# RMSNorm with Silu on one core: program order pinned on every engine, square-sums three tiles ahead, every fourth square-sum on VectorE

## The chip, the core and the metric

The kernel runs on one core of one Trainium2 chip. The metric is the device time of one execution in microseconds (us); the median of three runs is given. The core's engines used here are ScalarE (ACT in the profile), VectorE (DVE), GpSimd (POOL) and SyncE (SP), whose queue issues all transfers between device memory (HBM) and the on-chip memory (SBUF). TensorE does nothing in this kernel.

## The reference

```python
# x: (8, 1024, 2048) float32, gamma: (2048,) float32, eps: float32(1e-5)
rms = np.sqrt(np.mean(x ** 2, axis=-1, keepdims=True) + eps)
out = gamma * x / rms
return (out * (1 / (1 + np.exp(-out)))).astype(np.float32)
```

Each row of 2048 numbers is divided by its root mean square, multiplied by gamma and passed through Silu. Input and output are 67 MB each.

## The kernel before

The 8192 rows are cut into 64 tiles of 128 rows by 2048 columns, float32, 1 MB each. A tile lives in one buffer of a pool `xt` of 23 buffers from its load to its store: it is scaled and passed through Silu in place.

For a tile i there are four steps.

- `load(i)` (line 41) issues a DMA from x to a buffer on SP's queue.
- `stats(i)`: line 59 is a Square on ScalarE, which writes the squares to a scratch tile `sq` that nobody reads and accumulates the row sums into `ss` (on the chip this is the activation and a small accumulator read behind it). Lines 61 and 64 on GpSimd turn the row sum into `var` = mean + eps and `rstd` = var to the power of -0.5; both work on a single column of 128 numbers.
- `scale(i)` (line 68) is one VectorE instruction over the whole tile: x times `rstd` times `g`, in place. `g` is gamma copied to all 128 partitions by GpSimd at the start (line 47).
- `finish(i)`: line 73 is the Silu on ScalarE, in place; line 74 issues the store of the tile on SP's queue; then `load(i+16)` is issued on the same queue.

Sixteen loads are issued at first (`LEAD` = 16). The main loop's turn i calls `stats(i)`, `scale(i-1)` and `finish(i-2)`. The order in which each engine receives its instructions is not this order as written: a scheduler in the framework places them, with the program's dependences as its limits, and each engine then works through its own list in order. The engines wait for one another by semaphores.

Of the kernel before, what the change touches and what calls it, by code (L numbers as in the profile page):

```python
# [1 line left out]

# [4 lines left out]

ACT = mybir.ActivationFunctionType
ALU = mybir.AluOpType


@with_exitstack
def kernel(
    ctx: ExitStack,
    tc: tile.TileContext,
    x: bass.AP,
    gamma: bass.AP,
    eps: bass.AP,
    out: bass.AP,
):  # L20


    nc = tc.nc
    P = nc.NUM_PARTITIONS
    bf16 = mybir.dt.bfloat16
    f32 = mybir.dt.float32
    x2 = x.flatten_outer_dims()
    o2 = out.flatten_outer_dims()
    n, d = x2.shape
    ntiles = n // P  # L30
    BUFS, LEAD = 23, 16

    singles = ctx.enter_context(tc.tile_pool(name="singles", bufs=1))
    pool = ctx.enter_context(tc.tile_pool(name="pool", bufs=BUFS))
    small = ctx.enter_context(tc.tile_pool(name="small", bufs=8))

    xts = {}

    def load(i):
        xt = pool.tile([P, d], f32, name="xt")  # L40
        nc.sync.dma_start(out=xt, in_=x2[i * P:(i + 1) * P])
        xts[i] = xt

    grow = singles.tile([1, d], f32)
    nc.sync.dma_start(out=grow, in_=bass.AP(tensor=gamma.tensor, offset=gamma.offset, ap=[[d, 1], gamma.ap[0]]))
    g = singles.tile([P, d], f32)
    nc.gpsimd.partition_broadcast(g, grow)  # L47
    half = singles.tile([P, 1], f32)
    nc.gpsimd.memset(half, -0.5)  # L49
    sq = singles.tile([P, d], bf16)  # L50

    for i in range(LEAD):
        load(i)

    rstds = {}

    def stats(i):
        ss = small.tile([P, 1], f32, name="ss")
        nc.scalar.activation(out=sq, in_=xts[i], func=ACT.Square, accum_out=ss)  # L59
        var = small.tile([P, 1], f32, name="var")  # L60
        nc.gpsimd.tensor_scalar(out=var, in0=ss, scalar1=1.0 / d, scalar2=float(eps),  # L61
                                op0=ALU.mult, op1=ALU.add)
        rstd = small.tile([P, 1], f32, name="rstd")
        nc.gpsimd.tensor_tensor(out=rstd, in0=var, in1=half, op=ALU.pow)  # L64
        rstds[i] = rstd

    def scale(i):
        nc.vector.scalar_tensor_tensor(out=xts[i], in0=xts[i], scalar=rstds.pop(i), in1=g,  # L68
                                       op0=ALU.mult, op1=ALU.mult)

    def finish(i):
        xt = xts.pop(i)
        nc.scalar.activation(out=xt, in_=xt, func=ACT.Silu)  # L73
        nc.sync.dma_start(out=o2[i * P:(i + 1) * P], in_=xt)
        if i + LEAD < ntiles:
            load(i + LEAD)

    for i in range(ntiles + 2):
        if i < ntiles:
            stats(i)  # L80
        if 0 <= i - 1 < ntiles:
            scale(i - 1)
        if i >= 2:
            finish(i - 2)


# [1 line left out]
_INS = ['x', 'gamma', 'eps']  # L88
_OUTS = [((8, 1024, 2048), 'float32')]

_NUMBERS = {'eps': 9.999999747378752e-06}


# [26 lines left out]
```

## Time and profile before

| | |
|---|---|
| median of 3 runs | 413.59 us (413.02 to 413.94) |
| the profiled execution | 412.76 us; its span from first to last instruction 410.8 us |
| ScalarE busy | 244.6 us, 60% of the span |
| VectorE busy | 150.4 us, 37% |
| GpSimd busy | 60.1 us, 15% |
| moved by DMA | 134.28 MB, mean 327 GB/s over the span |

The profile describes one execution. Its page cuts the span in 40 equal slices of 10.27 us; a digit is the busy share of an engine in that slice in tenths, and the row GB/s tells what the 16 DMA engines moved. A list of waits names who waited for whom, in total and at the longest; the timeline lists instructions by start, duration, engine, line and operation, with the idle time ahead of one in brackets, and what ended it. Times inside the profile count from the start of the span; an execution takes 1.96 us more than its span here (412.76 less 410.8).

### The profile page before, as it was taken

What the parts mean: (1) busy time and instruction counts of PE and PEld (TensorE: products, weight loads), DVE (VectorE), ACT (ScalarE), POOL (GpSimd) and SP (SyncE); (2) the same over time, 40 slices, a digit from 0 to 9 for tenths busy, and PEclk for the clock granted to TensorE, in tenths of its full rate; (3) what the DMA queues carried; (4) which work ended last, traced back from release to release, by engine and by line L of the source; (5) the groups of instructions that cost most, each with busy time, mean ns of one, the idle gap of its engine ahead of it and who ended that gap; (6) DMA issues with size and microseconds to landing.
All of it is one profiled execution on the core that took longest, in us unless ns stands there. A gap on an engine that the chain in (4) does not pass through costs nothing.

```text
span 410.8 us, 895 instructions
## 1 busy us (share of the span) xinstructions
DVE 150.4 (37%) x64; ACT 244.6 (60%) x194; POOL 60.1 (15%) x134
## 2 busy tenths in 40 slices
DVE  0067666634242323324424233232424233242422
ACT  4549999984636465554763645556463645546462
POOL 1176212210010101010201010101001010101100
DMA  7999999999999999999999987887844242424334
GB/s 308 419 424 422 416 426 427 425 428 426 427 428 427 428 426 428 427 428 428 428 427 428 365 303 298 300 312 281 295 179 165 112 194 102 204 102 166 140 136 171
DMA packets 18440, 134.28 MB, mean 327 GB/s; under 512 B 2049, under 2 KB 2049, under 8 KB 2049
## 3 DMA queue, kind: packets, MB, share of 16 engines
q1 hardware_dynamic: 18434, 134.23, 80.0%
q14 instruction: 6, 0.05, 0.0%
HBM read 67.12 MB, written 67.11 MB: 327 GB/s over the span
## 4 chain that ended last, share of the span: by engine, by line
issue 76%; POOL 10%; DVE 1%; ACT 0%; POOLq 0%
POOL rstd L64 7%; POOL var L61 3%; DVE xt L68 1%; ACT xt L73 0%; POOLq L64 0%; POOLq L115 0%; ACT sq L59 0%
## 5 line engine op out<-in xcount | busy, mean ns | idle before, releaser
L68 DVE SCALAR_TENSOR_TENSOR xt<-xt,rstd,g 128x2048 f32<-128x2048 f32 x64 | 150.4, 2352 | 253.7 <-POOL rstd L64 252.9
L73 ACT ACTIVATE xt<-xt 128x2048 f32<-128x2048 f32 x64 | 121.7, 1905 | 155.1 <-DVE xt L68 154.0
L59 ACT ACTIVATE sq<-xt 128x2048 bf16<-128x2048 f32 x64 | 121.2, 1894 | 5.7 <-DMA xt<-in_x_dram 5.6
L61 POOL TENSOR_SCALAR var<-ss 128x1 f32<-128x1 f32 x64 | 20.4, 319 | 327.6 <-ACT sq L59 316.1
L64 POOL TENSOR_TENSOR rstd<-var,half 128x1 f32<-128x1 f32 x64 | 37.0, 579 | 5.4 <-POOL var L61 0.2
L59 ACT ACTIVATION_READ_ACCUMULATOR sq<-xt 128x1 f32 x64 | 11.9, 186 | 0.0
L47 POOL PARTITION_BROADCAST g<-grow x1 | 2.3, 2302 | 8.2 <-issue 8.2
L59 ACT ACT_TABLE_LOAD x1 | 1.3, 1283 | 0.7 <-PEq L101 0.7
L73 ACT ACT_TABLE_LOAD x1 | 1.3, 1283 | 0.0
L49 POOL MEMSET half<- 128x1 f32 x1 | 0.1, 99 | 0.3 <-POOLq L101 0.3
L101 POOL MEMSET const-float32-0.0<- 128x1 f32 x1 | 0.1, 98 | 0.2 <-issue 0.2
L101 POOL MEMSET const-bfloat16-1.0<- 128x1 bf16 x1 | 0.1, 101 | 0.0
L101 POOL MEMSET const-uint8-127<- 128x1 uint8 x1 | 0.1, 101 | 0.0
L101 POOL MEMSET const-float32-1.0<- 128x1 f32 x1 | 0.1, 99 | 0.0
## 6 DMA issues: line engine op xcount, KB each, us to landing
xt<-in_x_dram SPq DMA_DIRECT2D x64, 1024.0 KB, 19.6
out_dram<-xt SPq DMA_DIRECT2D x64, 1024.0 KB, 18.2
grow<-in_gamma_dram SPq DMA_DIRECT2D x1, 8.0 KB
```

The costliest lines, as they stand in the source:

```text
L47: nc.gpsimd.partition_broadcast(g, grow)
L49: nc.gpsimd.memset(half, -0.5)
L59: nc.scalar.activation(out=sq, in_=xts[i], func=ACT.Square, accum_out=ss)
L61: nc.gpsimd.tensor_scalar(out=var, in0=ss, scalar1=1.0 / d, scalar2=float(eps), op0=ALU.mult, op1=ALU.add)
L64: nc.gpsimd.tensor_tensor(out=rstd, in0=var, in1=half, op=ALU.pow)
L68: nc.vector.scalar_tensor_tensor(out=xts[i], in0=xts[i], scalar=rstds.pop(i), in1=g, op0=ALU.mult, op1=ALU.mult)
L73: nc.scalar.activation(out=xt, in_=xt, func=ACT.Silu)
L101: nc = _bacc.Bacc("TRN2", target_bir_lowering=False, num_devices=1)
```

## The change

Everything from the load of gamma to the last store stands inside `tc.manual_schedule()`: each engine gets its instructions in the order of the program's text. The loop is rewritten: `stats` of tiles 0, 1, 2 come first, and turn i then calls `stats(i+3)`, `scale(i)`, `finish(i-1)`. In `stats`, tiles with i % 4 == 3 take their square-sum by one VectorE instruction, whose elementwise result goes to a scratch tile `junk` in PSUM; the others stay on ScalarE, with two scratch tiles `sq` in turn. For the second `sq` the pool `xt` has 22 buffers and `LEAD` is 15.

```diff
-    BUFS, LEAD = 23, 16
+    BUFS, LEAD = 22, 15
...
+    psum = ctx.enter_context(tc.tile_pool(name="psum", bufs=1, space=bass.MemoryType.PSUM))
...
+    with tc.manual_schedule():
...
-    sq = singles.tile([P, d], bf16)
+        sq = [singles.tile([P, d], bf16, name=f"sq{k}") for k in range(2)]
+        junk = psum.tile([P, d], f32)
...
         def stats(i):
             ss = small.tile([P, 1], f32, name="ss")
-        nc.scalar.activation(out=sq, in_=xts[i], func=ACT.Square, accum_out=ss)
+            if i % 4 == 3:
+                nc.vector.tensor_tensor_reduce(out=junk, in0=xts[i], in1=xts[i], scale=1.0, scalar=0.0,
+                                               op0=ALU.mult, op1=ALU.add, accum_out=ss)
+            else:
+                nc.scalar.activation(out=sq[i % 2], in_=xts[i], func=ACT.Square, accum_out=ss)
...
-    for i in range(ntiles + 2):
-        if i < ntiles:
+        for i in range(3):
             stats(i)
-        if 0 <= i - 1 < ntiles:
-            scale(i - 1)
-        if i >= 2:
-            finish(i - 2)
+        for i in range(ntiles):
+            if i + 3 < ntiles:
+                stats(i + 3)
+            scale(i)
+            if i >= 1:
+                finish(i - 1)
+        finish(ntiles - 1)
```

The code of `var`, `rstd`, `scale` and `finish` is the same, further to the right. On GpSimd's queue the text puts the broadcast of gamma ahead of the memset of `half`.

More of the change, by code (lines that the diff above doesn't have):

```diff
@@ L42, in load @@
         xts[i] = xt
[L44 to L49, printed above, removed]
-    sq = singles.tile([P, d], bf16)
[L52 to L76, printed above, removed]
-    for i in range(ntiles + 2):
-        if i < ntiles:
-            stats(i)
-        if 0 <= i - 1 < ntiles:
-            scale(i - 1)
-        if i >= 2:
-            finish(i - 2)
+    with tc.manual_schedule():
+        grow = singles.tile([1, d], f32)
+        nc.sync.dma_start(out=grow, in_=bass.AP(tensor=gamma.tensor, offset=gamma.offset, ap=[[d, 1], gamma.ap[0]]))
+        g = singles.tile([P, d], f32)
+        nc.gpsimd.partition_broadcast(g, grow)
+        half = singles.tile([P, 1], f32)
+        nc.gpsimd.memset(half, -0.5)
+        sq = [singles.tile([P, d], bf16, name=f"sq{k}") for k in range(2)]
+        junk = psum.tile([P, d], f32)
+        for i in range(LEAD):
+            load(i)
+        rstds = {}
+        def stats(i):
+            ss = small.tile([P, 1], f32, name="ss")
+            if i % 4 == 3:
[3 more added lines that the diff above has]
+                nc.scalar.activation(out=sq[i % 2], in_=xts[i], func=ACT.Square, accum_out=ss)
+            var = small.tile([P, 1], f32, name="var")
+            nc.gpsimd.tensor_scalar(out=var, in0=ss, scalar1=1.0 / d, scalar2=float(eps),
+                                    op0=ALU.mult, op1=ALU.add)
+            rstd = small.tile([P, 1], f32, name="rstd")
+            nc.gpsimd.tensor_tensor(out=rstd, in0=var, in1=half, op=ALU.pow)
+            rstds[i] = rstd
+        def scale(i):
+            nc.vector.scalar_tensor_tensor(out=xts[i], in0=xts[i], scalar=rstds.pop(i), in1=g,
+                                           op0=ALU.mult, op1=ALU.mult)
+        def finish(i):
+            xt = xts.pop(i)
+            nc.scalar.activation(out=xt, in_=xt, func=ACT.Silu)
+            nc.sync.dma_start(out=o2[i * P:(i + 1) * P], in_=xt)
+            if i + LEAD < ntiles:
+                load(i + LEAD)
+        for i in range(3):
+            stats(i)
+        for i in range(ntiles):
[5 more added lines that the diff above has]
+        finish(ntiles - 1)
```

## The prediction

> **What bounds the kernel now.** I read the page's slices first, then a table by stretches of time, then the waits and the timeline of one stretch, then the SP queue.
>
> ```profile
> span 410.8 us, 895 instructions
> GB/s 308 419 424 422 416 426 427 425 428 426 427 428 427 428 426 428 427 428 428 428 427 428 365 303 298 300 312 281 295 179 165 112 194 102 204 102 166 140 136 171
> DMA packets 18440, 134.28 MB, mean 327 GB/s; under 512 B 2049, under 2 KB 2049, under 8 KB 2049
> ...
> 0.00:10.27 10.27, 0.00 (x0) 4.92 (x4) 1.56 (x6) 1.00 0.78 308
> 10.27:84.00 73.73, 42.23 (x18) 63.23 (x54) 23.70 (x38) 1.00 1.01 423
> 84.00:226.00 142.00, 49.39 (x21) 79.49 (x63) 16.40 (x42) 1.00 1.01 427
> 226.00:300.00 74.00, 23.52 (x10) 40.72 (x32) 7.37 (x20) 1.00 0.84 304
> 300.00:411.00 111.00, 35.28 (x15) 56.19 (x45) 11.06 (x30) 1.00 0.37 151
> ```
>
> The rows of stretches give length, busy time of VectorE, ScalarE and GpSimd, clock, DMA share and GB/s. Up to 226 us the 16 DMA engines are full at 423 to 428 GB/s. After that they are not: 304, then 151. So the first 226 us are bound by transfers and the last 185 us by something else; ScalarE, busy 40.72 of 74 us and 56.19 of 111, isn't it.
>
> ```profile
> 277.69 1.89 ACT L59 ACTIVATE sq<-xt 128x2048 bf16<-128x2048 f32 x1
> 279.49 0.19 ACT L59 ACTIVATION_READ_ACCUMULATOR sq<-xt 128x1 f32 x1
> 279.77 0.19 POOL L61 TENSOR_SCALAR var<-ss 128x1 f32<-128x1 f32 x1 [6.31 <-ACT sq L59]
> 280.04 0.55 POOL L64 TENSOR_TENSOR rstd<-var,half 128x1 f32<-128x1 f32 x1
> 280.62 2.35 DVE L68 SCALAR_TENSOR_TENSOR xt<-xt,rstd,g 128x2048 f32<-128x2048 f32 x1 [4.78 <-POOL rstd L64]
> 283.01 1.91 ACT L73 ACTIVATE xt<-xt 128x2048 f32<-128x2048 f32 x1 [3.33 <-DVE xt L68]
> 284.82 1.89 ACT L59 ACTIVATE sq<-xt 128x2048 bf16<-128x2048 f32 x1
> ```
>
> This is a ring: Square, var, rstd, scale, Silu, and only behind that Silu the next tile's Square. It turns in 284.82 - 277.69 = 7.13 us, each engine waiting for the one before it. The scheduler's order does it: the Silu of a tile stands on ScalarE directly behind that tile's own Square. The waits from 84 us on, a query over that stretch, agree:
>
> ```profile
> DVE xt L68 <- POOL rstd L64: 212.5, 46, 4.9
> ACT xt L73 <- DVE xt L68: 144.5, 44, 3.5
> ```
>
> The ring sets the pace from 84 us on, but until 226 us transfers queued ahead hide it. Before 84 us another order held, in which ScalarE never waited and a tile took 3.7 us (rows below).
>
> **The change, part by part.**
>
> *The new order.* ScalarE gets Square(i+3), then Silu(i-1). Silu(i-1) depends on a Square issued four turns earlier, so the ring is open and each engine can run at its own rate. That rate, from these rows:
>
> ```profile
> 32.04 1.89 ACT L73 ACTIVATE xt<-xt 128x2048 f32<-128x2048 f32 x1
> 33.84 1.89 ACT L59 ACTIVATE sq<-xt 128x2048 bf16<-128x2048 f32 x1
> 35.74 1.89 ACT L73 ACTIVATE xt<-xt 128x2048 f32<-128x2048 f32 x1
> ...
> L68 DVE SCALAR_TENSOR_TENSOR xt<-xt,rstd,g 128x2048 f32<-128x2048 f32 x64 | 150.4, 2352 | 253.7 <-POOL rstd L64 252.9
> ```
>
> From start to start a Silu takes 33.84 - 32.04 = 1.80 us and a Square 35.74 - 33.84 = 1.90. Per four tiles ScalarE then has 4 x 1.80 + 3 x 1.90 = 12.9 us, 3.23 a tile (3.70 with all Squares).
>
> *The square-sum on VectorE.* No row shows this operation, nor VectorE writing PSUM. Bounds: 1.90 us (the same work on ScalarE) and 4.70 (two passes as long as a scale). I take 2.35, the scale, which also reads two full float32 operands on the same engine. VectorE then has 4 x 2.35 + 2.35 = 11.8 us per four tiles, 2.94 a tile; with the upper bound 3.53.
>
> *GpSimd beside VectorE.* These two block each other:
>
> ```profile
> 28.74 2.35 DVE L68 SCALAR_TENSOR_TENSOR xt<-xt,rstd,g 128x2048 f32<-128x2048 f32 x1 [0.44 <-POOL rstd L64]
> 28.79 2.35 POOL L61 TENSOR_SCALAR var<-ss 128x1 f32<-128x1 f32 x1
> 31.23 0.55 POOL L64 TENSOR_TENSOR rstd<-var,half 128x1 f32<-128x1 f32 x1
> ```
>
> A `var` of 0.19 us took 2.35 beside a scale. At worst the two engines work strictly in turn: 2.94 + 0.19 + 0.55 = 3.68 us a tile (4.27 with the upper bound). Scale(i) needs an rstd whose square-sum is three turns old, so a `var` that waits out one VectorE instruction delays nothing.
>
> *Transfers.* A tile is two transfers of 1.049 MB; at 427 GB/s 2 x 2.456 = 4.91 us. That is above 3.23, 2.94, 3.68 and 4.27: the transfers become the bound all the way, if SP always has the next one to issue. Its queue:
>
> ```profile
> 1.12 23.27 SPq L41 DMA_DIRECT2D xt<-in_x_dram  x16
> 13.61 1.91 ACT L59 ACTIVATE sq<-xt 128x2048 bf16<-128x2048 f32 x1 [0.47 <-DMA xt<-in_x_dram]
> 22.52 0.45 POOL L61 TENSOR_SCALAR var<-ss 128x1 f32<-128x1 f32 x2 [11.22 <-issue]
> 23.69 4.61 DVE L68 SCALAR_TENSOR_TENSOR xt<-xt,rstd,g 128x2048 f32<-128x2048 f32 x2 [23.69 <-POOL rstd L64]
> 26.07 1.91 ACT L73 ACTIVATE xt<-xt 128x2048 f32<-128x2048 f32 x1 [9.16 <-DVE xt L68]
> 28.01 0.34 SPq L74 DMA_DIRECT2D out_dram<-xt  x1
> ...
> SPq L74 <- ACT xt L73: 203.4, 34, 6.7
> SPq L41 <- DMA xt<-in_x_dram: 80.0, 40, 2.7
> ...
> xt<-in_x_dram SPq DMA_DIRECT2D x64, 1024.0 KB, 19.6
> ```
>
> A load lands 19.6 us after its issue, 8 x 2.456: eight transfers are under way at a time, and SP waits for the oldest. Now the places where it could run dry.
>
> At the start the path to the first store is unchanged: it hangs on GpSimd's first `var` at 22.52, before which nothing that the profile shows holds it back, and I keep that start. Scale(0) follows at 23.7, Silu(0) at 26.07, store(0) at 28.01. The new VectorE square-sum of tile 3, ahead of scale(0), starts when its load lands near 13.6 and is done by 16 (18.3 by the upper bound). Square(4), ahead of Silu(0), is done near 18. Moving the memset of `half` behind the broadcast costs 0.1 us under that same gap: nothing. One load fewer: load 14 lands at 13.6 + 11 x 2.456 = 40.6, so the DMA engines have work until then and the first store comes 12.6 us sooner. From there a pair of store and load is offered each 3.7 us and eaten each 4.91: the queue is back at eight within some 25 us.
>
> In the steady state load(i+15), issued behind store(i), lands eight transfers later, about when store(i+4) is issued. Silu(j) follows Square(j+4) on ScalarE, so it runs when load(j+4) is there; load(j+4) went out behind store(j-11) and lands about at store(j-7). Store(j) is thus ready some six pairs, 29 us, before its turn. The store's wait, behind which the next load is queued on SP, costs nothing; if that cover went, it would be the 203.4 us row again. A load reuses the buffer of tile i-7, whose store was issued 15 transfers earlier and landed with eight under way. So 22 buffers cost nothing, nor does the second `sq`: Squares follow in order on one engine anyway.
>
> At the end load(63) lands with 15 stores to go, 36.8 us of transfers. VectorE then does its square-sum and four scales, 11.8 us, then Silu(63), 1.9: some 14 us after the landing, with up to 3 for GpSimd 17. Store(63) may be issued at 7 x 2.456 = 17.2. Covered, and eight under way give another 19.6.
>
> *The sum.* From the stretches: 308 x 10.27 + 423 x 73.73 + 427 x 142 = 95.0 MB by 226 us, at the full rate already. The remaining 39.3 MB at 427 GB/s take 92.0 us: 318.0. The last store of before shows what follows the last byte:
>
> ```profile
> 409.00:409.50 0.50, 0.00 (x0) 0.00 (x0) 0.00 (x0) 1.00 0.67 279
> 409.50:410.00 0.50, 0.00 (x0) 0.00 (x0) 0.00 (x0) 1.00 0.01 0
> DMA to landing us min/median/max: 3.9/3.9/4.0
> ```
>
> Bytes stop near 409.5, the span ends at 410.8: 1.3 us. So the span is 319.3 and the execution 1.96 more, 321.3. The profiled execution, 412.76, lies 0.83 under the median: 322. With 423 GB/s after 84 us instead of 427, 99.9 MB take 2.2 us more; with 430, 1.6 less.
>
> The DMA row against a rule: 428 GB/s stood for slice after slice. The Trainium skill, DMA: Bandwidth & Descriptors, section Where 436 GB/s comes from, says that for transfers between HBM and SBUF the HBM side binds, at about 358 GB/s for a core. By that the whole would take an estimated 375 us of transfer, some 381 in all; the trace, at 427 with loads and stores mixed, disagrees.
>
> **Rivals.**
>
> *A. Stores alone are slower.* The last 15 stores run without loads. A lone store lands 3.9 us after issue (row above); 15 of those instead of 2.456 add 21.7 us: 344. This would show as slices near 270 GB/s at the end. Against it: between its first and last byte it moved at full rate, and the initial loads, alone, ran at 419 to 424. 4%.
>
> *B. The rate isn't held when all engines work.* The lowest row with a nearly full queue is 365 GB/s, in the slice where it ran dry. The remaining 39.3 MB at that rate take 107.7 us: 338; all at 365: about 375. Against it: 10.27 to 84 us, with ScalarE 86% busy, still gave 423. 3%. The skill's rule just named would end here, at about 381.
>
> *C. VectorE becomes the bound.* In strict turns with GpSimd, a tile passes 4.91 us once the square-sum exceeds 4 x 4.91 - 4 x (2.35 + 0.74) = 7.3 us. Each us above costs 16 us; at 10 us the time is 322 + 43 = 365. For it: no row times this operation. 3%.
>
> *D. Slower: SP's queue goes one at a time.* With the order pinned, a load stands behind a store that waits for a Silu. Were each transfer to wait for the one before to land, a pair would take at least 2 x 3.9 = 7.8 us: 64 x 7.8 = 499. It decides from 6.3 us a pair, 64 x 6.3 = 403. Against it: SP's waits for loads are 2.0 us each (80.0 in 40), less than one transfer. 2%.
>
> *E. The ring stays.* If ScalarE still got a tile's Silu right behind its Square, the pace of 7.13 us and 413 us would stay. Against it is only that the text's order is what each engine gets. 1%.
>
> **How the numbers follow.** The forecast has 87%, A to E 4, 3, 3, 2 and 1. The forecast's own span is 319 to 326: transfer rate 430 to 423, start and end a few us worse. 318 to 330 leaves out the rivals and little else. A measurement can tell about 0.2% (0.8 us; the runs of before spread by that much). Faster 97%, within 0.2% 1%, slower 2%.
>
> **What would show it.** GB/s near 425 in every slice from the second to the last but one; ScalarE about 69% busy (48 Squares, 64 Silus), waiting mostly for loads; VectorE 64 scales and 16 square-sums near 2.35 us, 188 us or near 59%; SP waiting for DMAs in nearly every wait and hardly for Silu; the ring's two waits of 6.31 and 4.78 us gone. The prediction is wrong if GB/s sags late (A, B), if the square-sum takes over 7 us (C), or if SP waits for Silu (D, E).

## The result, and the profile after

The changed kernel takes 323.58 us (median of four runs, 323.25 to 323.70) against 413.30 for the kernel before beside it (412.90 to 413.94): a ratio of 0.783, 95% interval 0.781 to 0.784. The forecast was 322, range 318 to 330. The profiled execution has a span of 321.8 us, 2.5 more than the 319.3 of the sum.

From the page of the changed kernel: span, busy rows, slices, queue.

```profile
span 321.8 us, 812 instructions
DVE 183.8 (57%) x96; ACT 213.2 (66%) x162; POOL 185.5 (58%) x134
...
GB/s 273 428 415 424 399 426 428 428 423 428 426 432 424 425 427 432 424 426 427 433 426 426 427 430 428 425 428 429 428 425 428 428 431 424 428 426 432 424 428 233
...
q1 hardware_dynamic: 18434, 134.23, 99.2%
```

All slices but the first and the last stand between 399 and 433 GB/s, and all but two of these at 423 or more; the 18 low slices at the end of the kernel before are gone. The queue's packets fill 99.2% of the 16 DMA engines' span (80.0% before). The kernel is bound by transfers over nearly the whole span; how it ends is taken up below.

The waits of the engines, and below them those of SP's queue (total us, times, longest):

```profile
DVE junk L64 <- DMA xt<-in_x_dram: 88.7, 11, 13.6
ACT sq L67 <- DMA xt<-in_x_dram: 61.6, 30, 4.2
...
DVE xt L76 <- POOL rstd L72: 22.5, 25, 7.3
ACT xt L81 <- DVE xt L76: 17.1, 10, 6.2
...
SPq L82 <- DMA out_dram<-xt: 118.5, 56, 2.9
SPq L43 <- DMA xt<-in_x_dram: 110.5, 54, 2.7
...
SPq L82 <- ACT xt L81: 7.5, 6, 3.6
```

The ring's waits have shrunk from 252.9 to 22.5 us (scale for rstd) and from 154.0 to 17.1 (Silu for scale). VectorE and ScalarE now wait mostly for loads. SP waited 203.4 us for Silus before and waits 7.5 now; otherwise it waits some 2 us each time for the oldest of the transfers under way.

The groups by line:

```profile
L76 DVE SCALAR_TENSOR_TENSOR xt<-xt,rstd,g 128x2048 f32<-128x2048 f32 x64 | 147.9, 2349 | 22.5 <-POOL rstd L72 22.5
L69 POOL TENSOR_SCALAR var<-ss 128x1 f32<-128x1 f32 x64 | 100.4, 1569 | 91.5 <-DVE ss L64 39.3
L64 DVE CUSTOM_DVE_ANT_0 junk<-xt 128x2048 f32<-128x2048 f32 x16 | 36.8, 2298 | 88.7 <-DMA xt<-in_x_dram 88.7
L64 DVE DVE_READ_ACCUMULATOR2_ANT ss<- 128x1 f32 x16 | 2.3, 142 | 0.0
```

The square-sum on VectorE takes 2.30 us and 0.14 for reading the accumulator. A `var` on GpSimd, 0.32 us on average before, takes 1.57 now, since most of them run beside an instruction of VectorE. VectorE's whole wait for `rstd` is 22.5 us, and the transfers, not VectorE, set the pace, so that costs next to nothing here.

### The profile page after: what moved, and what is told of

Read it like the earlier page. It is cut to its first block, busy times and chain, and to the rows that moved or that the text cites. A ratio compares the mean times of both kernels' runs of the same rounds, so it can differ in the third digit from the quotient of the medians.

```text
span 321.8 us, 812 instructions
## 1 busy us (share of the span) xinstructions
DVE 183.8 (57%) x96; ACT 213.2 (66%) x162; POOL 185.5 (58%) x134
## 3 DMA queue, kind: packets, MB, share of 16 engines
q1 hardware_dynamic: 18434, 134.23, 99.2%
## 5 line engine op out<-in xcount | busy, mean ns | idle before, releaser
L76 DVE SCALAR_TENSOR_TENSOR xt<-xt,rstd,g 128x2048 f32<-128x2048 f32 x64 | 147.9, 2349 | 22.5 <-POOL rstd L72 22.5
L69 POOL TENSOR_SCALAR var<-ss 128x1 f32<-128x1 f32 x64 | 100.4, 1569 | 91.5 <-DVE ss L64 39.3
L67 ACT ACTIVATE sq<-xt 128x2048 bf16<-128x2048 f32 x48 | 91.4, 1904 | 65.9 <-DMA xt<-in_x_dram 61.6
L81 ACT ACTIVATE xt<-xt 128x2048 f32<-128x2048 f32 x64 | 120.0, 1897 | 17.1 <-DVE xt L76 17.1
L64 DVE CUSTOM_DVE_ANT_0 junk<-xt 128x2048 f32<-128x2048 f32 x16 | 36.8, 2298 | 88.7 <-DMA xt<-in_x_dram 88.7
L72 POOL TENSOR_TENSOR rstd<-var,half 128x1 f32<-128x1 f32 x64 | 82.5, 1290 | 5.3
L67 ACT ACTIVATION_READ_ACCUMULATOR sq<-xt 128x1 f32 x48 | 8.9, 186 | 0.0
L64 DVE DVE_READ_ACCUMULATOR2_ANT ss<- 128x1 f32 x16 | 2.3, 142 | 0.0
```

The source lines that it names most:

```text
L64: nc.vector.tensor_tensor_reduce(out=junk, in0=xts[i], in1=xts[i], scale=1.0, scalar=0.0, op0=ALU.mult, op1=ALU.add, accum_out=ss)
L67: nc.scalar.activation(out=sq[i % 2], in_=xts[i], func=ACT.Square, accum_out=ss)
```

## The experiments

**How much of the gain is the order, and how much the square-sums taken off ScalarE?** The order alone:

```diff
-            if i % 4 == 3:
+            if False:
```

> All 64 square-sums stay on ScalarE; the order and everything else is the changed kernel's. Theory 'order': ScalarE at 1.80 + 1.90 = 3.70 us a tile is still faster than the two transfers of a tile at 4.91 us, so the time is that of the changed kernel, 323 to 325 us. Rival 'relief': if a part of the gain came from the 16 square-sums taken off ScalarE, the time goes up by up to 16 x 1.9 = 30 us, to 330 to 354 us.

Measured: 323.05 us (322.81 to 323.19), ratio 0.782 (0.780 to 0.783) to the kernel before. The rival falls: nothing of the gain is lost without the square-sums on VectorE. ScalarE is 76% busy, has 64 Squares again, and still waits for loads:

```profile
ACT sq L67 <- DMA xt<-in_x_dram: 43.2, 39, 4.0
```

The square-sums alone, in the kernel before, with its scheduler:

```diff
...
-        nc.scalar.activation(out=sq, in_=xts[i], func=ACT.Square, accum_out=ss)
+        if i % 4 == 3:
+            nc.vector.tensor_tensor_reduce(out=junk, in0=xts[i], in1=xts[i], scale=1.0, scalar=0.0,
+                                           op0=ALU.mult, op1=ALU.add, accum_out=ss)
+        else:
+            nc.scalar.activation(out=sq, in_=xts[i], func=ACT.Square, accum_out=ss)
```

> The kernel before with nothing changed but every fourth square-sum on VectorE; the scheduler places the instructions. By its list, Silu stands directly behind its own tile's Square from tile 16 on, as before, save for the tiles of VectorE. Theory 'order': the ring stays at 7.13 us for three tiles of four; for the fourth, from scale to the next Silu's end are 2.3 + 0.1 + 0.75 + 2.35 + 1.9 us, of which 1.9 lie beside the previous Silu, 5.5 us. A mean of 6.7 us a tile over 46 tiles: about 395 us (385 to 410). Rival 'relief': ScalarE's load was the matter, time under 350 us.

Measured: 407.47 us (407.30 to 410.61), ratio 0.989 (0.985 to 0.993). The rival falls: with ScalarE's busy share down from 60% to 53%, the time falls by 1.1%. The ring is there; the Silus of the timeline:

```profile
305.39 1.91 ACT L80 ACTIVATE xt<-xt 128x2048 f32<-128x2048 f32 x1 [3.33 <-DVE xt L75]
...
312.52 1.91 ACT L80 ACTIVATE xt<-xt 128x2048 f32<-128x2048 f32 x1 [3.33 <-DVE xt L75]
...
318.09 1.91 ACT L80 ACTIVATE xt<-xt 128x2048 f32<-128x2048 f32 x1 [3.66 <-DVE xt L75]
...
325.23 1.91 ACT L80 ACTIVATE xt<-xt 128x2048 f32<-128x2048 f32 x1 [3.33 <-DVE xt L75]
```

7.13, 5.57 and 7.14 us, as worked out (7.13 and 5.5). The time lies inside the stated 385 to 410, but my 395 stopped at the last Silu's start and counted 46 steps. In the trace the ring takes 47 steps of 6.73 us on average, from the Silu at 82.53 to the last at 398.99; that Silu, its store and 2 us outside the span add 8.5.

**Does pinning do it, or the lead, and how much lead?** Three pinned loops, all square-sums on ScalarE, which differ only in how many tiles a Square is ahead of the Silu. No lead:

```diff
...
+        for i in range(ntiles):
+            stats(i)
+            scale(i)
+            finish(i)
```

> Pinned, all square-sums on ScalarE, no lead: each Silu stands directly behind its own tile's Square. Theory 'order': the ring of 7.13 us from the first tile to the last: first Silu done near 27.6 us, 63 x 7.13 = 449 more, then the last store, 4.7, and 2 outside the span: about 484 us, slower than the kernel before, which had the ring only from 84 us on. Rival 'pinning': if pinned order by itself, or the buffers, made the gain, 323 us.

Measured in one run: 483.82 us, slower than the kernel before by 17%, against "about 484". Two successive Silus of its timeline, 7.13 us apart:

```profile
304.21 1.91 ACT L81 ACTIVATE xt<-xt 128x2048 f32<-128x2048 f32 x1 [3.33 <-DVE xt L76]
...
311.34 1.91 ACT L81 ACTIVATE xt<-xt 128x2048 f32<-128x2048 f32 x1 [3.33 <-DVE xt L76]
```

One tile of lead:

```diff
...
+        for i in range(ntiles + 1):
+            if i < ntiles:
+                stats(i)
+                scale(i)
+            if i >= 1:
+                finish(i - 1)
```

> Pinned, all square-sums on ScalarE, only one tile of lead: Square(j+1) stands ahead of Silu(j). Between the end of Square(j) and Silu(j) lie Silu(j-1) and Square(j+1), 3.7 us, against var, rstd and scale, 0.9 + 2.4 = 3.3 us. Theory 'order': no ring above 4.91 us a tile, 323 to 326 us. Rival 'three tiles are needed': a pace above 4.91, thus over 330 us.

Two, with the loop's text of the kernel before inside the pinned block:

```diff
...
+        for i in range(ntiles + 2):
+            if i < ntiles:
+                stats(i)
+            if 0 <= i - 1 < ntiles:
+                scale(i - 1)
+            if i >= 2:
+                finish(i - 2)
```

> The loop's text is that of the kernel before (stats(i), scale(i-1), finish(i-2)), pinned; all square-sums on ScalarE; Square(j+2) stands ahead of Silu(j). Theory 'order': the text of before was enough, the ring came from the placing: 323 to 325 us. Rival 'three tiles are needed': var and rstd of a tile each wait behind a scale (2 x 2.4 us), so with two tiles of lead a part of the ring stays and the time is over 330 us.

Measured: 322.97 us (322.65 to 323.79) with one tile, 322.90 (322.82 to 323.03) with two. So pinning without a lead gains nothing, one tile of lead is worth the whole gain, and the second and third bring nothing more. The text of the kernel before had a lead of two; its scheduler gave it away, which a row of the timeline of before shows:

```profile
83.74 5.49 ACT L73 ACTIVATE xt<-xt 128x2048 f32<-128x2048 f32 x3
```

Three Silus in a row at 83.7 us: until there a Square ran two tiles ahead; from there each Silu stands directly behind its own tile's Square, but for one tile near 200 us. Pinning, then, is what keeps the lead that the text has. Whether the scheduler would have kept the three tiles of the changed text was not tried.

**What hides the stores' waits: the depth of loads.**

```diff
-    BUFS, LEAD = 22, 15
+    BUFS, LEAD = 22, 5
```

> Only 5 loads ahead instead of 15. Then the load of tile i+4 is issued behind Silu(i-1) and the next Square but one waits for it. Theory 'depth': a new ring of Silu 1.9, issue 0.7, load 4.9 to 6.9, Square 1.9, 9.4 to 11.4 us a tile, a little less where VectorE has the Square: 540 to 700 us. Theory 'no depth needed': 323 us.

Measured in one run: 636.78 us. The engines' largest waits:

```profile
DVE junk L64 <- DMA xt<-in_x_dram: 438.1, 16, 29.2
ACT sq L67 <- DMA xt<-in_x_dram: 397.8, 48, 12.3
```

All 64 square-sums (16 and 48) now wait for their load, and each load but the first five stands on SP's queue behind a store that waits for a Silu; it is the very next Square, not the next but one, that needs it. Theory 'depth' holds. This is the queue order that rival D feared, but not D's condition: store and load are issued some 0.4 us apart (305.66 and 306.05 in the timeline), so a load does not wait for the store to land. With 15 loads ahead the same order costs nothing: SP waited 7.5 us for Silus in the whole changed kernel.

**When does VectorE become the bound?**

```diff
-            if i % 4 == 3:
+            if True:
```

> All 64 square-sums on VectorE, everything else as changed. Theory 'strict turns' of the prediction (VectorE and GpSimd never work beside each other): 2.35 + 2.30 + 0.14 + 0.74 = 5.53 us a tile, above the transfers' 4.91: 64 x 5.53 + 23 + some 7 = 384 us. Theory 'GpSimd slips in between': var and rstd each wait out one VectorE instruction but hold none up, so a tile takes 2.28 + 2.30 + 0.14 = 4.7 us: 323 to 326 us.

Measured: 344.39 us (342.92 to 345.17), ratio 0.833 (0.831 to 0.836): neither. One tile of its timeline:

```profile
148.84 2.35 DVE L76 SCALAR_TENSOR_TENSOR xt<-xt,rstd,g 128x2048 f32<-128x2048 f32 x1 [0.38 <-POOL rstd L72]
148.89 2.35 POOL L69 TENSOR_SCALAR var<-ss 128x1 f32<-128x1 f32 x1
151.11 2.29 DVE L64 CUSTOM_DVE_ANT_0 junk<-xt 128x2048 f32<-128x2048 f32 x1
151.32 2.48 POOL L72 TENSOR_TENSOR rstd<-var,half 128x1 f32<-128x1 f32 x1
153.32 0.14 DVE L64 DVE_READ_ACCUMULATOR2_ANT ss<- 128x1 f32 x1
153.84 2.35 DVE L76 SCALAR_TENSOR_TENSOR xt<-xt,rstd,g 128x2048 f32<-128x2048 f32 x1 [0.38 <-POOL rstd L72]
```

`var` lasts until the scale ends, `rstd` until the square-sum does, and the next scale waits 0.38 us for `rstd`: 5.00 us a tile, 0.09 above the transfers. The first scale starts at 23.95 us and the 61st, 60 x 5.00 later, at 323.69; the last three have no square-sum beside them and come 3.07 apart, and a Silu and a store bring the span to 341.9. The 7.3 us of rival C are for one square-sum in four tiles; with one in every tile, 2.44 us are enough to make the chain of VectorE and GpSimd the bound.

**Where did the missing 2.5 us go?** The end of the changed kernel, rows of stretches (length, busy VectorE, ScalarE and GpSimd, clock, DMA share, GB/s):

```profile
316.00:317.00 1.00, 0.00 (x0) 0.00 (x0) 0.00 (x0) 1.00 1.08 459
317.00:318.00 1.00, 0.00 (x0) 0.00 (x0) 0.00 (x0) 1.00 0.64 270
318.00:319.00 1.00, 0.00 (x0) 0.00 (x0) 0.00 (x0) 1.00 0.31 131
319.00:320.00 1.00, 0.00 (x0) 0.00 (x0) 0.00 (x0) 1.00 0.12 49
320.00:320.50 0.50, 0.00 (x0) 0.00 (x0) 0.00 (x0) 1.00 0.08 33
```

The DMA share falls from 317 on to two thirds, a third and less; 0.08 of 16 engines is about one. So the engines don't end together, and the last works until between 320.0 and 320.5. The bytes that are left at 317 are 0.47 MB, 1.1 us at 427 GB/s: with all engines at work to the end they would be over at 318.1, which is where the sum has them. The kernel with no computation:

```diff
-            nc.scalar.activation(out=xt, in_=xt, func=ACT.Silu)
...
         for i in range(ntiles):
...
+            finish(i)
```

> All arithmetic on the tiles is left out: the kernel stores what it loads, with the same loads, buffers and queue order. Theory 'transfers bound': 321 to 324 us, the same as the changed kernel to within its first store; the end of the span is as ragged as the changed kernel's (rate falling from 317 us, last byte 3.4 us later). Rival 'the computation costs the missing 2 us': 319.5 to 321.5 us with an end in which the bytes stop within 1 us.

Measured: 321.78 us (321.64 to 321.83), span 319.9. Its end:

```profile
316.00:317.00 1.00, 0.00 (x0) 1.00 1.00 426
317.00:318.00 1.00, 0.00 (x0) 1.00 0.39 164
318.00:319.00 1.00, 0.00 (x0) 1.00 0.04 16
```

Here only GpSimd's column is left, and the bytes are over by about 318.5. Neither theory holds as written. The time lies in the range of 'transfers bound' (321 to 324) and not in the rival's; the end falls off over 1.5 us, nearer to the rival's 1 than to the 3.4 of the other. So the transfers alone need 321.8 us, 0.6 us of span more than the sum gave, and the longer ragged end, with it the other 1.9 us of span, comes with the computation. Does it come by the traffic of the computation, or by its instructions? The same instructions on 8 of the 2048 columns:

```diff
+                nc.vector.tensor_tensor_reduce(out=junk[:, :8], in0=xts[i][:, :8], in1=xts[i][:, :8], ...
...
+                nc.scalar.activation(out=sq[i % 2][:, :8], in_=xts[i][:, :8], func=ACT.Square, accum_out=ss)
...
+            nc.vector.scalar_tensor_tensor(out=xts[i][:, :8], in0=xts[i][:, :8], scalar=rstds.pop(i), in1=g[:, :8],
...
+            nc.scalar.activation(out=xt[:, :8], in_=xt[:, :8], func=ACT.Silu)
```

> Same instructions, waits and transfers as the changed kernel, but every instruction on the tiles works on 8 of 2048 columns; the rest of the arithmetic is left out. The copy alone ended 1.8 us before the changed kernel, most of it in its last slice. Theory 'instruction fetch': the six packets of the instruction queue (8 KB each, against one in the copy) delay single DMA engines, so the end stays ragged, 323 to 324 us. Theory 'memory traffic of the computation': the full-width instructions disturb the transfers, so this kernel ends like the copy, 321.5 to 322.2 us.

Measured: 323.52 us (322.99 to 323.79), beside 323.40 (323.39 to 323.86) for the changed kernel, run again in the same set:

> The changed kernel once more, beside the two others of this set: 323.3 to 323.8 us, span near 321.8, bytes falling off from 317 us and ending near 320.4.

So it is not the traffic of the full width. A last kernel lets these small instructions work on four scratch tiles w of 8 columns, so that no transfer waits for them:

```diff
+        w = [singles.tile([P, 8], f32, name=f"w{k}") for k in range(4)]
...
-            nc.scalar.activation(out=xt, in_=xt, func=ACT.Silu)
+            nc.scalar.activation(out=w[i % 4], in_=w[i % 4], func=ACT.Silu)
```

> The copy alone (321.78 us) with all the small instructions of the eight-column kernel beside it, but working on four scratch tiles of 8 columns, so that no load or store waits for them; the arithmetic on x is left out. It tells apart why the eight-column kernel (323.52 us) is 1.7 us over the copy. Theory 'instruction fetch': the same instructions bring the same packets of the instruction queue, 323 to 324 us. Theory 'the tie': the later first store and the waits of the stores make the difference, 321.6 to 322.2 us.

Measured: 322.98 us (322.86 to 323.10), between the two theories and next to the first. So 1.2 of the 1.7 us come with instructions that merely run beside the transfers. (The copy and this kernel stood in different sets of runs; the kernel before took 413.18 and 413.22 us in them.) The row of the instruction queue, first the changed kernel's, then the copy's, then this kernel's:

```profile
q14 instruction: 6, 0.05, 0.0%
```

```profile
q14 instruction: 1, 0.01, 0.0%
```

```profile
q14 instruction: 4, 0.03, 0.0%
```

That these packets, 8 KB each, hold up single DMA engines fits these three, but their number alone doesn't give the time: the kernels with one and two tiles of lead have six packets too, and take some 0.5 us less than the changed one. The timelines say more. SP issues a transfer when the oldest of eight has landed, so a late landing shows as a late issue. Rows of the copy, then of the last kernel:

```profile
23.33 0.35 SPq L81 DMA_DIRECT2D out_dram<-xt  x1
...
40.82 0.33 SPq L43 DMA_DIRECT2D xt<-in_x_dram  x1
```

```profile
24.10 0.35 SPq L86 DMA_DIRECT2D out_dram<-xt  x1
...
42.48 0.33 SPq L43 DMA_DIRECT2D xt<-in_x_dram  x1
```

The first store is 0.77 us behind that of the copy, before any packet of the instruction queue: the span up to 40 us has none, the first three come between 40 and 60. At 42.48 us the lag is 1.66. The last small instruction ends at 84 us, and still the bytes fall off from 317 to 320 us: 344, 139 and 66 GB/s. So the lag arises early and most of it stays to the end.

The trace also keeps when each of the 16 parts of a transfer lands, though no view prints it. Over a run the parts of one transfer drift apart, and while the queue is full they hardly come together again. In the profiled executions, the distance between the first and the last part of the last store to land goes nearly in the order of the times:

| kernel | parts of the last store, us apart | median time, us |
|---|---|---|
| copy | 1.65 | 321.78 |
| small instructions on scratch tiles | 2.34 | 322.98 |
| one, two, three tiles of lead, square-sums on ScalarE | 2.44, 2.69, 2.76 | 322.97, 322.90, 323.05 |
| changed kernel on 8 columns | 3.36 | 323.52 |
| changed kernel, both times | 3.51, 3.36 | 323.58, 323.40 |

The drift grows in steps. In the changed kernel it is 0.6 us for the first five loads, 1.1 from the sixth, 1.5 from the fifteenth and 2.0 at 72 us, all before its first packet. Then it grows by 0.6, 0.3 and 0.7 within some 3 us of the packets at 89.2, 104.2 and 287.8 us; the other three (81.1, 127.8 and 223.4) leave no growth. In the copy it is 0.5 to 0.7 us until its only packet at 175.0, and 0.6 more behind it. So the packets do go with steps, in the changed kernel for about half of the drift. What makes the steps before the first packet, which the copy doesn't have, stays open; so does why the same number of packets makes 0.5 us more where VectorE has square-sums.

**Can the first bytes come sooner?** The kernel with two tiles of lead, and in it:

```diff
-        nc.sync.dma_start(out=grow, ...
+        nc.scalar.dma_start(out=grow, ...
```

> The kernel with two tiles of lead and all square-sums on ScalarE (322.90 us), with the load of gamma issued by ScalarE's queue instead of SP's, so that the first load of x is issued at 0.7 instead of 1.1 us. Theory 'transfers bound from the first byte': 0.3 to 0.5 us less, 322.4 to 322.6 us. Rival: the first bytes wait for something else than the issue, 322.9 us as before.

Measured: 322.88 us (322.70 to 323.05) beside 323.40 for the changed kernel, ranges that don't overlap. But the kernel with two tiles of lead had 322.90 without this edit. The first load is issued 0.4 us earlier; the end doesn't come sooner. So the rival holds. The 0.5 us or 0.16% under the changed kernel go with leaving the square-sums on ScalarE, not with this edit.

## Why the prediction was right, point by point

- *The ring bounds the kernel before from 84 us on.* Shown from both sides: with no lead 483.8 us, where a sum made of the ring and its two ends gave 484; with one tile of lead 323.
- *The transfers are the next bound, at 427 GB/s for loads and stores mixed.* Shown: 99.2% of the DMA engines' time, and the copy alone takes 321.8. The Trainium skill, DMA: Bandwidth & Descriptors, section Where 436 GB/s comes from, has the HBM side bind near 358 GB/s a core; the trace disagrees, with 427 or 428 in every stretch of 50 us from 60 to 310 us. The Trainium skill's HBM Reference, section Specifications (TRN2), says that a core streaming alone gets about 425: with that the trace agrees.
- *The stores' waits are covered.* In the trace of the changed kernel a store is ready 28 us or more before SP issues it, from tile 24 to tile 49 (forecast: 29). At the end 13.3 us pass from the start of the last square-sum to the end of the last Silu (forecast: 14 to 17), and that store still waits 4.6 us for its turn.
- *Stores alone run at full rate* (against rival A): the last load has landed by 283.6 us, where the last square-sum starts, and the slices behind that, but for the very last, stand at 424 to 432 GB/s. Rival B falls with the same row.
- *VectorE's square-sum at 2.35 us*: 2.30 + 0.14 = 2.44. Busy 57% against 59 forecast, ScalarE 66% against 69: the durations add up to 187.0 and 222.9 us, about as forecast, but successive instructions of an engine overlap a little, so that the busy time is 183.8 and 213.2.
- *Strict turns of VectorE and GpSimd*: too strict as a bound. GpSimd waits for nearly all of it, VectorE for little; all 64 square-sums on VectorE gave 5.00 us a tile and not 5.53. Here it made no difference. The Trainium skill, SBUF — State Buffer, section SBUF: two separate sides, says that a VectorE instruction with two SBUF inputs that starts first blocks a GpSimd instruction that reads SBUF until it ends; the 2.35 us of `var` beside the scale agree, and with 8 columns, where VectorE's instructions are 0.2 us, `var` is back at 0.197.
- *The start is kept.* The first store is issued at 27.58 us (28.01 before). It doesn't bind: the kernel on 8 columns issues it at 24.19 us and takes as long.
- *The remaining 39.3 MB at 427 GB/s, to 318.0 us.* This is the term that was mis-sized. It takes the 16 engines to work at the full rate to the last byte. The only end that the prediction had looked at, the last store of before, had them end together: its parts land 0.16 us apart. But that store stood alone; in the full queue of before the parts had come 2.4 us apart by 220 us, and they came together only when the queue ran dry. After 314 us of full queues the engines of the changed kernel end one by one over some 3.5 us, the last near 320.5: 2.5 us that the sum doesn't have. The term behind it, 1.3 us from the last byte to the end of the span, was right (321.8 less 320.5).
- *322 against 323.58* looks nearer than it is. The forecast adds 0.83 us because the median of before lay above its profiled run; this time the two differ by 0.07. That luck hides 0.9 of the 2.5 us.

The change does several things, and only one of them earned its time. The second and third tile of lead bring nothing measurable. The 16 square-sums on VectorE gain nothing and seem to cost some 0.5 us: the changed kernel took 323.58 and 323.40 us, the four pinned kernels with a lead and without these square-sums 322.88 to 323.05. That is 0.16%, inside the 0.2% that one measurement can tell. The second scratch tile, the 22 buffers and the 15 loads ahead were in all pinned kernels but one, which had 5 loads, so they were not tried by themselves.

## What to carry to other kernels

Where neither an engine nor the transfers are full, and the engines wait for one another in many short waits, look for a ring: write one tile's instructions in order of time and see whether the first of the next tile stands behind the last of this one. One tile of distance may open it, and the pace then falls to the next bound, which can be computed beforehand from bytes and the rate that the full slices show. An order left to a scheduler can lose such a distance in the middle of a run, so read the timeline in more than one place.

## What was not expected of the hardware

Beside full DMA queues, some 460 more instructions (636 against 178 in all) that touch none of the transferred data came with 1.2 us more (321.78 against 322.98 us). They are over at 84 us, and the lag that arose by 43 us still shows at the end, some 275 us later: the 16 parts of a transfer drift apart (0.3 us at first, 2.3 at the end) and don't come together again while the queue is full. And two engines that exclude each other do not simply add up: with a square-sum of VectorE in every tile, GpSimd's small instructions end at VectorE's boundaries, one per VectorE instruction, and VectorE pays 0.38 us a tile and not 0.74.
